# First layer's MLP over both token halves, and the last MLP's first matrix, by seven block products

## The chip, the cores and the metric

One NeuronCore of a Trainium2 chip runs the whole program. The metric is the device time in microseconds (us), here the median of three runs. In the text PE is TensorE (matmuls, weight loads as PEld), DVE is VectorE, ACT is ScalarE, POOL is GpSimd and SP the engine that issues the DMAs.

## The reference

A decoder trunk of two layers over 1024 tokens of width 1024, in float32: an mLSTM layer, then a latent-attention layer, each followed by an MLP of width 4096 with a squared ReLU. Only the MLP and its surroundings are changed:

```python
def sqrelu_mlp(h, w1, w2):
    return jnp.square(jax.nn.relu(h @ w1)) @ w2
...
    for l in range(DEPTH):
        ada = cond @ ada_w[l] + ada_b[l]
        sh1, sc1, g1, sh2, sc2, g2 = jnp.split(ada, 6, axis=-1)
        h = modulate(rmsnorm(x, norm_g[l, 0]), sh1, sc1)
        ...                       # y: the layer's mixer of h (mLSTM or attention)
        x = x + g1[:, None, :] * rmsnorm(y, norm_g[l, 1])
        h = modulate(rmsnorm(x, norm_g[l, 2]), sh2, sc2)
        y = sqrelu_mlp(h, mlp_w1[l], mlp_w2[l])
        x = x + g2[:, None, :] * rmsnorm(y, norm_g[l, 3])
```

## The kernel before, in words

The tokens are worked on in two halves of 512. Activations lie feature-major: a tile holds 128 features on the partitions and 512 tokens along the free dimension. A float32 product is made of three matmuls on parts: each operand is split into a rounded part (hi, type float32r) and the rest (lo), and `mm3` (L230 to L233) issues lo x hi, hi x lo and hi x hi into the same PSUM bank. Weights are loaded by SP into a `raw` buffer of [128, 1024] (four of them), ACT copies the hi part and DVE subtracts for the lo part (`wsplit`, L189 and L190, eight `ws` buffers). Most activations live in 24 `k4` and 8 `hd` buffers of the same size.

`mlp` (from L941) makes one MLP for one half. A hidden column block `f` (32 of 128 columns) takes 8 x 3 matmuls of 512 columns over K = 1024, then ReLU and square on ACT (L957, L958) and a split into hi and lo (`split_mod`, L470 and L471). The second matrix follows behind in groups of G hidden blocks (`up_cols`, or `up_rows`, where the result is wanted with tokens on the partitions), summed into the result in SBUF by DVE (`accumulate`, L198). Steps of both matrices alternate; weights are loaded two steps ahead (AHEAD). A step of 24 matmuls is cut by a "within" in the middle.

The order in time is: mLSTM of both halves; `post`, which adds the residual, takes the norm and leaves the modulated `hf.h2` in parts; then the layer's MLP of half 0, that of half 1 beside the attention of half 0, the last MLP of half 0 beside the attention of half 1, and the last MLP of half 1 alone. `two_streams` weaves them: the mixer yields how many dense steps are to run before it goes on (0.5 is half a step, 12 matmuls; "align" waits for a step of the first matrix), so the yields are the cover behind which a chain of vector work may run. `go` fixes the order of PE's instructions as written; the other engines and the DMA queue are ordered by the scheduler of the framework, by priority (`PRIO` lifts weight loads and evacuations) and by its own estimate of time. Background work (adaLN products `ada_chunk`, rotary tables, latent weights) is stepped from generators: `bgs`, `bg_latent` and `bg_rest`.

Of the kernel before, what the change touches and what calls it, by code (L numbers as in the profile page):

```python
# [9 lines left out]
F32 = mybir.dt.float32  # L10
# [72 lines left out]
def kernel(  # L83
# [145 lines left out]

    def mm3(o, lh, ll, rh, rl, start, stop):  # L230
        nc.tensor.matmul(o, ll, rh, start=start, stop=False)  # L231
        nc.tensor.matmul(o, lh, rl, start=False, stop=False)  # L232
        pe_last[0] = nc.tensor.matmul(o, lh, rh, start=False, stop=stop)  # L233

# [241 lines left out]
    def normed(h, xs_, rstd, A, sh):  # L476

        for k in range(KD):
            with paced():
                nc.vector.scalar_tensor_tensor(  # L480
                    xs_[k], xs_[k], A[:, k : k + 1], rstd, ALU.mult, ALU.mult
                )
                split_mod(h.hi[k], h.lo[k], xs_[k], sh[:, k : k + 1])
            if k % 4 == 3:
                yield 1

# [453 lines left out]

    def mlp(l, hf, y, sizes, rows=False):  # L941


        w1, w2, h = mlp_w1[l], mlp_w2[l], hf.h2
        hids = {}

        def hidden(f):
# [25 lines left out]
        def up_rows(fs, i, last):  # L973
# [40 lines left out]
            def out(ws):  # L1014
                for t in range(t0, t1):
                    if t % 2 == 0:
                        if t > t0:
                            yield "within"
                        b2 = pm()
                    block(b2[:, t % 2], ws, t)  # L1020
# [6 lines left out]
        def up_cols(fs, i, last):  # L1027
# [3 lines left out]
            def out(w):  # L1031
                for m in range(i * n, (i + 1) * n):
                    if m % 2 == 0:
                        if m > i * n:
                            yield "within"
                        b2 = pm()
                    pt = b2[:, m % 2]
                    for q, f in enumerate(fs):
# [6 lines left out]

        up = up_rows if rows else up_cols
        steps, prev, f0 = [], [], 0
        for G in sizes:
# [8 lines left out]
        steps += [up(prev, i, True) for i in range(len(prev))]  # L1057
        ready = []
        for n in range(len(steps) + AHEAD):
            if n < len(steps):  # L1060
                ready.append(steps[n][0]())
            if n >= AHEAD:
                yield from steps[n - AHEAD][1](ready.pop(0))

                yield steps[(n - AHEAD + 1) % len(steps)][1].__name__

# [305 lines left out]
    def prepare_pair(p_, hf):  # L1372
# [61 lines left out]
    def attend(hf, groups, dense, behind=lambda: None):  # L1434
# [46 lines left out]
        us = begin()  # L1481
        yield 1
        while us:
# [4 lines left out]
            for n, work in enumerate(rounds):  # L1488
# [4 lines left out]
                if len(rounds) == 1:  # L1493
                    yield 1
                if n == len(rounds) - 1:
# [6 lines left out]
    def attention_first(hf):  # L1502
# [61 lines left out]
    def x_to_rows(half):  # L1564

        for k in range(KD):
            a, b = tmc(), tmc()
            nc.sync.dma_start(a, xs_blk(k, half))
            yield
            pt = pc()  # L1570
            for t in range(4):
# [178 lines left out]

    def post(hf, y, B, src, A, sh):
        yield from residual(y, hf.i, B, src, (2, 2)[hf.i])
# [3 lines left out]
        rstd = last_of(rs)  # L1756
        yield 0
        hf.h2 = Split()
        yield from normed(hf.h2, y, rstd, A, sh)
# [4 lines left out]
    )  # L1764
    p0 = post(hfs[0], y0, B0, x_ahead(k4v, True), A1, adac(0, SH2))
    so = split_o(hfs[1])
# [81 lines left out]


    p1 = post(hfs[1], y1, B0, x_ahead(hdv, True), A1, adac(0, SH2))  # L1850
    next(p1)
    z0 = FH(claim=True)
    Akv = Aq = B2 = A3 = B3 = None
# [36 lines left out]
    z1 = FH(claim=True)  # L1890
    ya = [None, None]

    def mixer1(hf, z, attention):
# [14 lines left out]
        yield 1  # L1908
        yield from post(hf, y, B2, x_cols, A3, adac(1, SH2))
# [6 lines left out]
    u1 = FH(claim=True)  # L1916

    def all_out():
        yield from x_to_rows(0)
        B3r = along_rows(B3)  # L1920
        yield
        yield from rows_out(hfs[0], u0, B3r)
        yield from x_to_rows(1)
# [39 lines left out]
```

## Time and profile before

| | |
|---|---|
| median of three runs | 2397.75 us (2396.41 to 2398.75) |
| the profiled execution, first to last instruction | 2395.7 us, which is 2.05 us under the median |
| granted TensorE clock, mean | 0.997 |
| DVE busy | 1550.3 us, 65% |
| ACT busy | 1054.9 us, 44% |
| GpSimd busy | 18.3 us, 91 instructions |
| matmuls | 11621 |
| DMA | 374.48 MB, mean 156 GB/s |

No separate time of the profiled execution is given beside its span; what lies around the span is taken as the difference to the median. Busy times of engines overlap each other. The span is cut into 40 slices of some 60 us each; a digit is the busy share in tenths. The busy time of PE counts overlapping matmuls once, so the spacing of matmuls is read from their starts in the timeline.

### The profile page before, as it was taken

How to read it: one execution, taken by the hardware profiler on the slowest of the kernel's cores; microseconds unless marked ns; L12 is line 12 of the kernel's file. 1: busy time of each engine (PE TensorE's matmuls, PEld its weight loads, DVE VectorE, ACT ScalarE, POOL GpSimd, SP SyncE). 2: the span in 40 equal slices, each digit the busy share in tenths (PEclk: the TensorE clock that was granted, in tenths of full speed). 3: DMA queues.
4: the chain of work that ended last, by engine and by line, in shares of the span. 5: the costliest groups of instructions: out<-in, count | busy, mean ns of one | idle time of the engine just before them, and what ended most of it. 6: DMA issues, size and time to landing. Idle time of an engine off the chain costs nothing.

```text
span 2395.7 us, 30518 instructions
## 1 busy us (share of the span) xinstructions
PE 2364.8 (99%) x11621; PEld 1945.5 (81%) x11621; DVE 1550.3 (65%) x2431; ACT 1054.9 (44%) x1712; POOL 18.3 (1%) x91
## 2 busy tenths in 40 slices
PE   7999999999999999999999999999999999999998
PEld 5888888788888887888888877888888888888886
DVE  6667866858656677877764867766566386353345
ACT  4355334655333454444444554344444353443333
POOL 1000000000000000000000000000000000000000
PEclk9999999999999999999999999999999999999999
DMA  8442654544654745545543444864424354354431
GB/s 310 148 143 81 192 178 134 165 132 150 189 171 152 243 138 179 159 160 186 168 137 114 153 162 153 260 240 133 139 97 150 105 167 128 101 189 140 144 99 62
DMA packets 377106, 374.48 MB, mean 156 GB/s; under 512 B 24355, under 2 KB 282464, under 8 KB 376960
## 3 DMA queue, kind: packets, MB, share of 16 engines
q1 hardware_dynamic: 376672, 372.44, 48.9%
q8 instruction: 91, 1.49, 0.3%
q14 instruction: 55, 0.45, 0.1%
q0 software_dynamic: 288, 0.10, 0.0%
HBM read 313.24 MB, written 59.24 MB: 155 GB/s over the span
## 4 chain that ended last, share of the span: by engine, by line
PE 91%; DVE 4%; DMA 3%; ACT 1%; issue 1%; SPq 0%; DVEq 0%; ACTq 0%
PE ps L231 17%; PE ps L232 17%; PE ps L233 17%; PE pm L231 10%; PE pm L232 10%; PE pm L233 10%; PE pc L1445 1%; PE pc L231 1%; PE pc L233 1%; PE pc L232 1%; PE pm L815 1%; PE pm L1331 1%; DMA raw<-in_mlp_w_dram 1%; DVE wl L190 1%; PE pm L1325 1%
## 5 line engine op out<-in xcount | busy, mean ns | idle before, releaser
L190 DVE TENSOR_TENSOR wl<-raw,wh 128x1024 fp32r<-128x1024 f32 (+2 forms) x366 | 438.7, 1202 | 449.5 <-ACT wh L189 442.3
L189 ACT CAST wh<-raw 128x1024 fp32r<-128x1024 f32 (+2 forms) x366 | 376.0, 1032 | 717.0 <-PE ps L231 392.2
L231 PE MATMUL ps<-k,wl 128*128 128x512 f32 x1528 | 611.0, 400 | 2.3 <-ACT k L671 1.4
L233 PE MATMUL ps<-k,wh 128*128 128x512 f32 x1528 | 601.0, 393 | 0.0
L232 PE MATMUL ps<-k,wh 128*128 128x512 f32 x1528 | 600.9, 393 | 0.0
L231 PEld LDWEIGHTS ps<-k,wl 128*128 128x128 f32 x1528 | 287.0, 188 | 69.7 <-issue 2.9
L233 PEld LDWEIGHTS ps<-k,wh 128*128 128x128 f32 x1528 | 287.0, 188 | 67.3 <-issue 0.5
L232 PEld LDWEIGHTS ps<-k,wh 128*128 128x128 f32 x1528 | 287.5, 188 | 63.6 <-issue 1.7
L198 DVE TENSOR_TENSOR k<-k,pm 128x512 f32<-128x512 f32 (+1 forms) x254 | 210.9, 859 | 107.0 <-PE pm L233 106.5
L231 PE MATMUL pm<-hd,wl 128*128 128x512 f32 x512 | 202.0, 394 | 0.4 <-ACT hd L470 0.4
L233 PE MATMUL pm<-hd,wh 128*128 128x512 f32 x512 | 199.8, 391 | 0.0
L232 PE MATMUL pm<-hd,wh 128*128 128x512 f32 x512 | 199.5, 390 | 0.2 <-DVE hd L471 0.2
L231 PE MATMUL pm<-wh,hd 128*128 128x512 f32 x488 | 192.9, 395 | 3.2 <-ACT raw L1337 2.9
L232 PE MATMUL pm<-wl,hd 128*128 128x512 f32 x488 | 191.3, 392 | 0.0
L233 PE MATMUL pm<-wh,hd 128*128 128x512 f32 x488 | 190.3, 390 | 0.0
L360 DVE SCALAR_TENSOR_TENSOR tma<-raw,cond,tma 128x512 f32<-128x512 f32 x168 | 125.6, 747 | 20.6 <-DMA raw<-in_kv_ada_w_dram 14.6
L471 DVE TENSOR_TENSOR hd<-tmp,hd 128x512 fp32r<-128x512 f32 x128 | 88.3, 690 | 56.8 <-ACT hd L470 56.5
L1337 ACT ACTIVATE raw<-pm,sm 128x128 f32<-128x128 f32 (+3 forms) x64 | 47.5, 742 | 151.3 <-DVE sm L1336 122.7
L232 PEld LDWEIGHTS pm<-hd,wh 128*128 128x128 f32 x512 | 96.2, 188 | 21.3 <-DVE hd L471 0.5
L231 PEld LDWEIGHTS pm<-hd,wl 128*128 128x128 f32 x512 | 96.1, 188 | 21.2 <-ACT hd L470 0.8
L233 PEld LDWEIGHTS pm<-hd,wh 128*128 128x128 f32 x512 | 96.1, 188 | 21.1
L231 PEld LDWEIGHTS pm<-wh,hd 128*128 128x128 f32 x488 | 91.6, 188 | 24.9 <-ACT raw L1337 5.5
(347 smaller groups left out, 3414.5 us busy)
## 6 DMA issues: line engine op xcount, KB each, us to landing
raw<-in_mlp_w_dram SPq DMA_DIRECT2D x256, 512.0 KB, 4.1
raw<-in_ada_w_dram SPq DMA_DIRECT2D x80, 512.0 KB, 4.3
raw<-in_a_w_in_dram SPq DMA_DIRECT2D x48, 512.0 KB, 4.1
xs<-k SPq DMA_DIRECT2D x40, 256.0 KB, 4.8
raw<-in_kv_ada_w_dram SPq DMA_DIRECT2D x16, 512.0 KB, 3.8
raw<-in_a_w_out_dram SPq DMA_DIRECT2D x16, 512.0 KB, 4.6
kd<-k SPq DMA_DIRECT2D x32, 256.0 KB, 3.7
vd<-k SPq DMA_DIRECT2D x32, 256.0 KB, 5.0
```

The lines of the kernel that those rows point to most:

```text
L189: nc.scalar.copy(hi[:, :n], r[:, :n])
L190: i = nc.vector.tensor_sub(lo[:, :n], r[:, :n], hi[:, :n].bitcast(F32))
L198: return f(*a, **k)
L231: nc.tensor.matmul(o, ll, rh, start=start, stop=False)
L232: nc.tensor.matmul(o, lh, rl, start=False, stop=False)
L233: pe_last[0] = nc.tensor.matmul(o, lh, rh, start=False, stop=stop)
L360: nc.vector.scalar_tensor_tensor(acc, r[:, kk], cond[:, k : k + 1], acc, ALU.mult, ALU.add)
L471: nc.vector.tensor_sub(lo, u, hi.bitcast(F32))
L815: nc.tensor.matmul(nv[:, r, i], hf.PT[p_][:, r, cs], v[:, 2 * p_ + r], start=g == 0, stop=True,)
L1325: nc.tensor.matmul(o[:, :w], ql, kh, start=True, stop=False)
L1331: nc.tensor.matmul(o[:, :w], qh, kh, start=False, stop=True)
L1337: nc.scalar.activation(pr[:, :n], f, AF.Exp, bias=m, scale=SCALE, accum_out=l)
```

## The change

The product of a 2 x 2 block matrix with another takes eight block products, or seven with sums of blocks before and after. The new `seven` does the latter for a pair of hidden column blocks: the weights' blocks are (two column blocks) x (two halves of K), the tokens' blocks are (two halves of K) x (two sets of tokens). Sums of the weights' blocks are made per pair in `load` by DVE (with `pool`, two of the four by GpSimd), sums of the tokens' blocks once beforehand. Each product is 4 x 3 matmuls; three of the sums afterwards are made by going on accumulating in the same PSUM bank, three by DVE with a copy that ACT kept.

- In layer 0 the two sets of tokens are the two halves (512 columns a matmul). The first ALONE = 6 pairs are still made one half at a time (`up_front`), for half 0 while half 1's `post` runs, for half 1 later, in the stream beside the first attention; the other ten pairs by `seven`, with background steps between the products. `kept0` and `kept1` keep the modulated values whole (`normed_kept`) and make the block sums.
- In the last MLP of half 1 the two sets are its two quarters (256 columns a matmul), all sixteen pairs; `quarters` makes the sums at the end of the attention's `post`.
- The hidden values of these three MLPs go to DRAM (`hidd`), and `mlp(..., stored=True)` then makes the second matrix as a phase of its own with groups of four, fetching and splitting two hidden blocks at a time. The last MLP of half 0 stays as it was.
- The yields of the first attention (`hf.i` = 0) are halved or cut, `bg_rest` runs behind `bg_latent` in the phases of layer 0, and `x_to_rows` of both halves moves into the last MLP's product phase, with its load one block ahead.

The diff, cut to its core:

```diff
+    def split_wide(hi, lo, u):
+        nc.scalar.copy(hi, u)
+        nc.vector.tensor_sub(lo, u, hi.bitcast(F32))
+    def normed_kept(y, rstd, A, sh, parts):
+        for b in range(4):
+            with paced():
+                for k in (2 * b, 2 * b + 1):
+                    nc.vector.scalar_tensor_tensor(
+                        y[k], y[k], A[:, k : k + 1], rstd, ALU.mult, ALU.mult
+                    )
+                    nc.scalar.activation(y[k], y[k], AF.Identity, bias=sh[:, k : k + 1])
+                if parts[b]:
+                    split_wide(*parts[b], y.t[b])
...
+    def up_front(l, hf, pairs):
...
+                s = tmp()
+                with tc.high_priority(PRIO):
+                    nc.scalar.activation(s, pt, AF.Relu)
+                    nc.scalar.activation(s, s, AF.Square)
+                    nc.sync.dma_start(hidd[hf.i, f // 2][:, ts(f % 2, 512)], s)
...
+    def seven(l, pairs, B, out, pool=False):
+        def load(p_):
+            with tc.high_priority(PRIO):
+                r1, r2 = raw(), raw()
+                for r, f in ((r1, 2 * p_), (r2, 2 * p_ + 1)):
+                    nc.sync.dma_start(r.rearrange("p (a b) -> p a b", b=P), wcols(w1, f * P))
+                lo_, hi_ = slice(0, 512), slice(512, 1024)
+                A = wsplit(r1, 1024)
+                t1, t2 = raw(), raw()
+                first = nc.gpsimd if pool else nc.vector
+                first.tensor_add(t2[:, lo_], r2[:, lo_], r2[:, hi_])
+                first.tensor_sub(t1[:, lo_], r1[:, lo_], r2[:, lo_])
+                nc.vector.tensor_sub(t1[:, hi_], t2[:, lo_], r1[:, lo_])
+                nc.vector.tensor_sub(t2[:, hi_], r1[:, hi_], t1[:, hi_])
+                T1 = wsplit(t1, 1024)
+                if pool:
+                    a22, T2 = hd(F32R), (hd(F32R), hd(F32R))
...
+                else:
+                    a22 = sb.tile([P, 1024], F32R, tag="ws", bufs=WS, name=f"wa_{next(uid)}")
+                    T2 = wsplit(t2, 1024)
+                nc.scalar.copy(a22[:, lo_], r2[:, hi_])
+                nc.vector.tensor_sub(a22[:, hi_], r2[:, hi_], a22[:, lo_].bitcast(F32))
...
+        def product(u, i):
+            o = {1: u.b, 6: u.b, 5: u.b, 3: u.b, 2: u.x, 7: u.z, 4: u.z}[i]
+            (wh, wl), (bh, bl) = u.w[i], B[i]
+            for k in range(4):
+                mm3(o, wh[:, k], wl[:, k], bh[k], bl[k], i in (1, 2, 7) and k == 0, k == 3, more=i not in (1, 2, 7))
...
+            for u, i in ((cur, 1), (prev, 5), (cur, 2), (prev, 4), (cur, 6), (prev, 3), (cur, 7)):
+                if u:
+                    product(u, i)
+                    yield "hid"
...
+        def fetch(f):
+            with tc.high_priority(PRIO):
+                r, hi, lo = raw(), k4v(F32R), k4v(F32R)
+                nc.sync.dma_start(r, hidd[hf.i, f // 2])
+                split_wide(hi, lo, r.rearrange("p (a b) -> p a b", b=512))
...
-        yield 1
+        yield (0.5, 1)[hf.i]                      # prepare_pair; the same twice in attend
...
-            yield 2
+            yield 1
...
-                hf, groups, cycle((1,)),
+                hf, groups, cycle((0.5,)),        # attention_first
...
-    f0 = mlp(0, hfs[0], z0, [4] * 8)
-    for n in range(20):
-        if next(f0) != "within":
+    for v in up_front(0, hfs[0], range(ALONE)):
+        if v != "within":
+            next(p1, None)
             next(p1, None)
     drain(p1)
-    two_streams(f0, behind(bg_latent(), 4))
+    bgl = chain(bg_latent(), bg_rest())
+    z0 = FH()
+    f2 = mlp(0, hfs[0], z0, [], stored=True)
+    f0, n = seven(0, range(ALONE, NF // 2), blocks, both_halves), 0
+    while go(f0) is not end:
...
+        next(bgl, None)
+        if n == 7 * (NF // 2 - ALONE) - 5:
+            next(f2)
...
+    two_streams(with_b12(f2), behind(bgl, 1))
...
-    two_streams(mlp(0, hfs[1], z1, [2] * 14 + [4]), mixer1(hfs[0], z0, attention_first), bg_rest())
+    two_streams(
+        chain(
+            up_front(0, hfs[1], range(ALONE)),
+            (v for v in mlp(0, hfs[1], z1, [], stored=True) if v != "primed"),
+        ),
+        mixer1(hfs[0], z0, attention_first), bgl,
+    )
...
-    dense = mlp(1, hfs[1], u1, [4] * 8, True)
+    dense, n = seven(1, range(NF // 2), blocks1, one_half(hfs[1]), True), 0
+    while go(dense) is not end:
+        n += 1
+        if n % 3 == 0 and v != "rows":
+            v = next(fill)
+    u1 = FH()
+    dense = mlp(1, hfs[1], u1, [], True, True)
```

More of the change, by code (lines that the diff above doesn't have):

```diff
@@ L228, with mm3 @@
     pe_last = [None]
[L230 to L233, printed above, removed]
+    def mm3(o, lh, ll, rh, rl, start, stop, more=False):
+        m = dict(skip_group_check=True) if more else {}
+        nc.tensor.matmul(o, ll, rh, start=start, stop=False, **m)
+        nc.tensor.matmul(o, lh, rl, start=False, stop=False, **m)
+        pe_last[0] = nc.tensor.matmul(o, lh, rh, start=False, stop=stop, **m)
     nc.scalar.preload_act_table_set("natural_log_exp_and_others")
@@ L939, with ahead_of @@
     AHEAD = 2
-    def mlp(l, hf, y, sizes, rows=False):
+    hidd = scratch([2, NF // 2, P, 2 * H], "hidd")
+    def ahead_of(steps, primed=False):
+        ready = []
+        for n in range(len(steps) + AHEAD):
+            if primed and n == AHEAD:
+                yield "primed"
+            if n < len(steps):
+                ready.append(steps[n][0]())
+            if n >= AHEAD:
+                yield from steps[n - AHEAD][1](ready.pop(0))
+                yield steps[(n - AHEAD + 1) % len(steps)][1].__name__
@@ L1046, in mlp, with both @@
         up = up_rows if rows else up_cols
+        if stored:
+            fetch(0)
+            fetch(2)
+            steps = []
+            for g in range(NF // 4):
+                for i in range(4):
+                    load, run = up(list(range(4 * g, 4 * g + 4)), i, g == NF // 4 - 1)
+                    def both(load=load, f=4 * g + 2 * i):
+                        w = load()
+                        if i >= 2 and f < NF:
+                            fetch(f)
+                        return w
+                    steps.append((both, run))
+            n = 0
+            for v in ahead_of(steps, True):
+                if v == "primed":
+                    yield v
+                    continue
+                n += v != "within"
+                yield v if v == "within" else "hid"
+            return
         steps, prev, f0 = [], [], 0
@@ L1057, in mlp @@
         steps += [up(prev, i, True) for i in range(len(prev))]
[L1058 to L1065, printed above, removed]
+        yield from ahead_of(steps)
     rope_d = scratch([2, P, S], "rope_d")
@@ L1481, in attend @@
         us = begin()
-        yield 1
+        yield (0.5, 1)[hf.i]
         while us:
@@ L1757, in post @@
         yield 0
+        if kept:
+            yield from kept(y, rstd)
+            return
         hf.h2 = Split()
```

207 lines of the change are left out of this document (194 added, 13 removed).

## The prediction, made before the run

> **What bounds the kernel now.** I read the page from its engines, over the forty slices, to the chain that ended last; then the groups of instructions with their shapes kept apart, then windows and the timeline where the change lands.
>
> ```profile
> PE 2364.8 (99%) x11621; PEld 1945.5 (81%) x11621; DVE 1550.3 (65%) x2431; ACT 1054.9 (44%) x1712; POOL 18.3 (1%) x91
> ...
> PE   7999999999999999999999999999999999999998
> ...
> PEclk9999999999999999999999999999999999999999
> ...
> PE 91%; DVE 4%; DMA 3%; ACT 1%; issue 1%; SPq 0%; DVEq 0%; ACTq 0%
> PE ps L231 17%; PE ps L232 17%; PE ps L233 17%; PE pm L231 10%; PE pm L232 10%; PE pm L233 10%; PE pc L1445 1%; PE pc L231 1%; PE pc L233 1%; PE pc L232 1%; PE pm L815 1%; PE pm L1331 1%; DMA raw<-in_mlp_w_dram 1%; DVE wl L190 1%; PE pm L1325 1%
> ```
>
> TensorE is busy 99% of the span at full granted clock, is 91% of the chain, and some 81% of the chain are the three matmul lines of mm3. So the time is a count of matmuls times their spacing, and a change pays by what it takes out of that count, less what it lets TensorE wait. The busy column can't give the spacing, since neighbours overlap; the timeline does, by starts.
>
> ```profile
> 317.16 0.28 PE L231 MATMUL ps<-wh,k 128*128 128x256 f32 x1
> ...
> 321.75 0.28 PE L231 MATMUL ps<-wh,k 128*128 128x256 f32 x1
> ...
> 1110.71 0.39 PE L231 MATMUL ps<-k,wl 128*128 128x512 f32 x1
> ...
> 1116.27 0.39 PE L231 MATMUL pm<-hd,wl 128*128 128x512 f32 x1
> ```
>
> From the third row to the fourth 24 matmuls of 512 columns start, 5.56 us, so 0.2317 us each. From the first to the second 39 matmuls of 256 columns start, 4.59 us, so 0.1177 us each, each with a weight load of its own: half as wide costs 51%.
>
> **The change: matmuls.** Layer 0's first matrix takes 2 x 768 matmuls of 512. After: six pairs of columns per half in the old way (2 x 288), ten pairs over both halves in seven products of 12 instead of eight (10 x 84 = 840); 1416 in all, 120 fewer, 120 x 0.2317 = 27.8 us. The last MLP's first matrix, 768 of 512 = 177.9 us, becomes 16 x 84 = 1344 of 256, x 0.1177 = 158.2 us: 19.7 us. Second matrices keep their 768 a piece. Together 47.5 us of TensorE's time. What follows is what the vector side charges for it.
>
> ```profile
> L190 DVE TENSOR_TENSOR wl<-raw,wh 128x1024 fp32r<-128x1024 f32 x350 | 426.6, 1222 | 444.5 <-ACT wh L189 440.1 <-PE ps L233 2.9 <-DMA lw<-wl 0.9
> L360 DVE SCALAR_TENSOR_TENSOR tma<-raw,cond,tma 128x512 f32<-128x512 f32 x168 | 125.6, 747 | 20.6 <-DMA raw<-in_kv_ada_w_dram 14.6 <-DMA raw<-in_ada_w_dram 4.3
> L198 DVE TENSOR_TENSOR k<-k,pm 128x512 f32<-128x512 f32 x170 | 108.9, 682 | 54.2 <-PE pm L233 53.7
> L471 DVE TENSOR_TENSOR hd<-tmp,hd 128x512 fp32r<-128x512 f32 x128 | 88.3, 690 | 56.8 <-ACT hd L470 56.5
> L457 DVE TENSOR_TENSOR tmc<-tmc,tmc 128x512 f32<-128x512 f32 x90 | 62.0, 689 | 7.1 <-ACT tmc L453 5.3
> L358 DVE TENSOR_SCALAR tma<-raw,cond 128x512 f32<-128x512 f32 x24 | 11.5, 478 | 3.8 <-DMA raw<-in_kv_ada_w_dram 3.6 <-DMA raw<-in_ada_w_dram 0.3
> L661 DVE COPY k<-ps 128x256 f32<-128x256 f32 x16 | 6.7, 420 | 5.1 <-PE ps L233 5.1
> L1339 DVE TENSOR_SCALAR raw<-raw,sm 128x1024 f32<-128x1024 f32 x8 | 6.0, 754 | 0.6
> ...
> L189 ACT CAST wh<-raw 128x1024 fp32r<-128x1024 f32 x350 | 365.3, 1048 | 708.4 <-PE ps L231 391.8 <-DMA raw<-in_mlp_w_dram 101.4 <-PE pm L231 80.4
> ...
> L612 POOL MEMSET raw<- 128x1024 f32 x2 | 1.9, 954 | 146.9 <-DVE wl L190 146.9
> ...
> raw<-in_mlp_w_dram SPq DMA_DIRECT2D x256, 512.0 KB, 4.1
> ```
>
> **Layer 0's ten pairs.** VectorE per pair: three weight splits (3 x 1.22), four block sums (4 x 0.69), the seventh block's rest (0.69), three adds out of PSUM (3 x 0.68), two ReLUs (0.75 + 0.48): 10.4 us. Seven steps of the background come beside it; a chunk of the adaLN product has seven steps and 0.48 + 7 x 0.75 = 5.7 us. So 16.1 us against 84 x 0.2317 = 19.5 us of TensorE, 83%.
>
> ```profile
> 495.00:566.00 71.00, 71.00 (x307) 57.25 (x306) 53.61 (x77) 42.20 (x61) 0.55 (x4) 1.00 0.44 139
> 960.00:1200.00 240.00, 239.21 (x1239) 200.03 (x1238) 185.83 (x325) 101.19 (x188) 2.87 (x14) 1.00 0.54 170
> 1560.00:1860.00 300.00, 295.69 (x1626) 250.82 (x1625) 186.40 (x304) 128.54 (x217) 3.60 (x20) 1.00 0.46 153
> 1920.00:1980.00 60.00, 60.00 (x263) 48.64 (x262) 55.90 (x81) 33.12 (x49) 0.20 (x2) 1.00 0.49 159
> ```
>
> (The columns are the window, its length, then busy time and count of PE, PEld, DVE, ACT and POOL, the clock, the DMA share, GB/s.) The last window had VectorE at 93% with TensorE never idle, so 83% is covered; I charge 2 us, between 0 and one 1.2 us instruction in the way in each of ten pairs.
>
> **Getting there.** The block sums of the tokens must be ready before the third product. The first column of the old first matrix starts at 492.38 in the trace and half 1's last square is added by 495.05:
>
> ```profile
> 492.38 0.39 PE L231 MATMUL ps<-k,wl 128*128 128x512 f32 x1
> ...
> 494.36 0.69 DVE L457 TENSOR_TENSOR tmc<-tmc,tmc 128x512 f32<-128x512 f32 x1
> ...
> 1124.94 0.36 PE L1331 MATMUL pm<-k,k 128*128 128x256 f32 x1
> ...
> 1128.92 0.35 DVE L1339 TENSOR_SCALAR raw<-raw,sm 128x256 f32<-128x256 f32 x1
> ...
> 1130.70 1.04 PE L1445 MATMUL pc<-ident,raw 128*128 128x128 f32 x8
> ```
>
> From there VectorE has two reciprocal roots (8 x 0.69), the residual (8 x 0.75 + 8 x 0.69), seven sums of squares (4.8), the norm (8 x 0.75) and eighteen wide operations of sums and splits (18 x 1.22): some 50 us; ten weight splits, 12 us; the first pair's weights, 3 x 1.22 + 5 x 0.69 = 7 us. That is 69 us, to 564. TensorE has twelve columns (12 x 5.56) and two products (5.6), to 565. It just fits if VectorE never idles; in the old chain's window, 495 to 566, it idled 17.4 of 71 us. So 0 to 16 us of waiting, and I take 6: the pacing of one step per column made part of the old idling, and the steps now come two per column.
>
> **Attention of half 0.** Its dense cover falls from 1536 matmuls to 1056, and most yields of the pairs are halved, so 12 matmuls (2.78 us) stand where 24 stood. In the first round of a pair the last score starts at 1124.94, the last scaling ends at 1129.27, and TensorE comes to the transposes at 1130.70; with 2.78 us less it comes at 1127.92 and waits 1.35 us. The second attention (1560 to 1860), which has half steps already, idles 4.3 of 300 us against 0.8 of 240 in the first. Four pairs with one such wait: 5.4 us, with three waits each 16 us, with VectorE relieved of G=2's extra adds perhaps none. I take 6. Its dense work also ends nearly with the mixer, so the norm ahead of the last layer's MLP loses cover: 2 us, at most one step's 5.6.
>
> **The last MLP's sixteen pairs.** Here a pair has only 84 x 0.1177 = 9.9 us. VectorE: three splits 3.67, two sums 1.38, the seventh block 0.69, three adds of 256 (3 x 0.42), one ReLU 0.75: 7.75 us, 78%. GpSimd has two sums of 512, an operation that the trace lacks; its write of 1024 took 0.95 us, so not under 0.48 us each, and I put the upper end at twice VectorE's 0.69. If they run beside VectorE nothing is lost; one after the other it is 8.7 to 10.5 us per pair, up to 0.6 over. I take 6 us for the stage, half of that and a little for the short slack of a product (1.4 us) against a 1.05 us ScalarE copy in the way.
>
> **Hidden by cover.** The hidden values' way through DRAM: 60 stores and 48 loads, about 50 MB on top of 374, and 20 weight loads fewer; the mean of 156 GB/s rises to about 175. A store lands tens of us before its load. The 48 wide splits after the load (59 us of VectorE) replace 96 splits of 0.69 at L471 (66 us).
>
> The sum: span 2395.7 - 47.5 + 2 + 6 + 6 + 2 + 6 = 2370.2; the span shown lies 2.05 under the median, so 2372 us.
>
> **Rivals.** (1) All new waits are hidden, as nearly all were before: 2397.75 - 47.5 = 2350 us. For it: the slices of nines. Against: the 1.35 us worked out above.
>
> (2) VectorE and GpSimd exclude each other in the last MLP. By rows: a two-input operation of VectorE stands still while GpSimd's runs and the other way round, so a pair costs 10.5 us and, with each delay passed on to the weight splits, up to 1.5 us over TensorE's 9.9: 24 us in place of 6, so 2390 us. Nothing in this trace shows it, as GpSimd here only writes. The Trainium skill, page "SBUF — State Buffer", section "Who interferes with whom", states just this: a VectorE instruction with two SBUF inputs and a GpSimd instruction that reads SBUF hold a shared port in turn, each for its whole length. No run here has tested it.
>
> (3) Slower: the weights of the last MLP's pairs become a chain. A pair needs all four raw buffers: two landings (4.1 us), GpSimd's two sums (1 to 2.8), two sums (1.4), then copy (1.05) and three splits in turn (1.22, 1.22, 0.69): 10.7 to 12.5 us from issue to the release of the second buffer. If the next pair's loads wait for that release, sixteen pairs at 12.5 cost 42 us over TensorE's 9.9, in place of 6: 2408 us. It decides from 12 us per pair on. Against: the first buffer is free after the sums, so two pairs can overlap.
>
> (4) A 256-column matmul is bound by its weights.
>
> ```profile
> L231 PEld LDWEIGHTS ps<-k,wl 128*128 128x128 f32 x1528 | 287.0, 188 | 69.7 <-issue 2.9
> ```
>
> At 0.188 us a load, 1344 would take 253 us and the kernel 2465. The 39 matmuls at 0.1177 speak plainly against it.
>
> **How the numbers follow.** Forecast 50%, its own range 2358 to 2385; (1) 20%; (2) 15%; (3) 13%; (4) 2%. The range 2345 to 2402 leaves out (4), most of (3)'s upper half, and what lies 5 us and more under (1), the vector work saved being no more than that in the places where TensorE waits. A measurement here tells 0.2%, 4.8 us, from no change: faster 0.83 (forecast, (1) and nearly all of (2)), same 0.05 (the edges of (2) and (3)), slower 0.12.
>
> **What would show it.** Matmul count down to some 12,080 (120 fewer of 512, 768 of 512 gone, 1344 of 256 new). The spacing of the new 256s at 0.118. Between two pairs of the last MLP 9.9 to 10.5 us; 12 or more speaks for (3), a VectorE two-input operation of 512 longer than 0.69 there for (2). An idle of TensorE ended by VectorE once at some 565 us, and of about 1.3 us ahead of L1445's successors in each pair of the first attention. I am wrong if the idle time of TensorE grows by over 47 us, or the 256s space out.

## The result, and the profile after

The changed kernel takes 2524.68 us (median of four runs, 2523.22 to 2532.22) against 2397.40 for the kernel before on the same chip: ratio 1.0531, 95% interval 1.0513 to 1.0548. It is 127 us slower where 25 us faster were forecast. The profiled execution took 2524.39 us, its span 2522.5. Here is its page: busy time by engine, the forty slices, the DMA total, the chain that ended last, and the costliest groups.

```profile
PE 2367.9 (94%) x12077; PEld 1961.3 (78%) x12077; DVE 1746.8 (69%) x2643; ACT 1129.4 (45%) x1770; POOL 64.5 (3%) x111
...
PE   8999999998996998798999989999999999898998
...
PEclk9999999999998999799999989999999999999999
...
DMA packets 386524, 441.71 MB, mean 175 GB/s; under 512 B 26595, under 2 KB 278560, under 8 KB 386368
...
PE 69%; DMA 13%; DVE 11%; ACT 3%; issue 3%; POOL 0%; SPq 0%; DVEq 0%; ACTq 0%; POOLq 0%
...
L490 DVE TENSOR_TENSOR k<-raw,k 128x1024 fp32r<-128x1024 f32 x98 | 119.6, 1224 | 95.7 <-ACT k L489 94.3
...
L489 ACT CAST k<-raw 128x1024 fp32r<-128x1024 f32 x98 | 102.5, 1050 | 143.6 <-DMA raw<-hidd 139.4
...
raw<-hidd SPq DMA_DIRECT2D x96, 512.0 KB, 4.4
```

Of the matmuls all came as forecast: 12077. (By the code four of the seven products, not three as the section on the change says, go on accumulating in a bank that another has begun.) The new ones of 256 columns have the spacing of the old: in the timeline twenty of them start from the first to the second row here, 2.35 us, 0.1175 each.

```profile
2199.80 0.28 PE L232 MATMUL ps<-k,wl 128*128 128x256 f32 x1
...
2202.15 0.28 PE L234 MATMUL ps<-k,hd 128*128 128x256 f32 x1
```

So the 47.5 us of matmul time are saved, and TensorE loses some 175 us more than before. Of these 124 are idle time (the span less PE's busy time: 30.9 us before, 154.6 after), where the prediction called itself wrong from 47 on. The rest lies within what the page counts as busy, in part as matmuls at a lower clock (last section). PE fell from 91% of the chain to 69%, and DMA and DVE stand there with 13% and 11%. The last row of the first fence is the one to remember: 96 loads of hidden values, where the prediction counted 48.

To place the loss, the timeline has a mark in each stage: the two matmuls with a tile of ones that sum the squares of a residual stream (L461 before, L462 after). The three marks below end the first layer's MLP of half 0, the first attention with the MLP of half 1, and the second attention. Before:

```profile
866.70 1.02 PE L461 MATMUL pc<-tmc,ones 128*128 128x512 f32 x2
...
1411.38 1.02 PE L461 MATMUL pc<-tmc,ones 128*128 128x512 f32 x2
...
1958.52 1.02 PE L461 MATMUL pc<-tmc,ones 128*128 128x512 f32 x2
```

After:

```profile
1048.59 1.02 PE L462 MATMUL pc<-tmc,ones 128*128 128x512 f32 x2
...
1520.20 1.02 PE L462 MATMUL pc<-tmc,ones 128*128 128x512 f32 x2
...
2067.13 1.02 PE L462 MATMUL pc<-tmc,ones 128*128 128x512 f32 x2
```

By the count of matmuls the first stage has 360 more of 512 (+83.4 us), the second 480 fewer (-111.2), the tail 19.7 us less. Loss is what lies over that:

| stage | before | by count | after | loss | forecast loss |
|---|---|---|---|---|---|
| to the first mark | 866.7 | 950.1 | 1048.6 | 98.5 | 8 |
| first attention | 544.7 | 433.5 | 471.6 | 38.1 | 8 |
| second attention | 547.1 | 547.1 | 546.9 | 0 | 0 |
| last MLP of half 1, to the end | 437.2 | 417.5 | 455.4 | 37.9 | 6 |

What TensorE waited for stands in the view of waits with TensorE's rows alone (columns: waiting matmul, releaser, us in total, times, longest). First the first stage, from 530 to 1048 us, a window in which TensorE is busy for 446.8 of 518 us (in the kernel before, for all of it):

```profile
PE pc L341 <- DVE tma L361: 22.0, 3, 8.4
PE pm L232 <- ACT k L202: 9.7, 1, 9.7
PE ps L232 <- DVE wl L190: 7.5, 3, 4.4
PE ps L233 <- DVE hd L490: 6.3, 1, 6.3
...
PE pc L1386 <- DVE tma L1378: 5.5, 1, 5.5
```

Then the first attention's, from 1049 to 1520:

```profile
PE pm L232 <- ACT k L489: 9.4, 2, 5.4
PE pm L232 <- ACT raw L1569: 8.4, 8, 1.3
PE pm L233 <- DVE k L490: 5.1, 2, 4.0
```

And the tail, from 2067 on:

```profile
PE pm L232 <- DVE hd L1042: 15.2, 12, 2.6
```

L341 and L1386 are transposes of background work (an adaLN vector, a bias of the latent weights): they stand in TensorE's queue, and no matmul ran past them, until VectorE had finished the sum that they transpose. L489 and L490 split a fetched pair of hidden values; L202 empties a PSUM tile, on ScalarE, which ahead of it had stood 7.2 us for a block of the background's weights (L1381) and then, at L489, 4.8 us for a fetch. L1042 is an addition of the last MLP's products.

### The profile page after: what moved, and what is told of

The parts are those of the page before. It is cut to its first block, busy times and chain, and to the rows that moved or that the text cites. A ratio compares the mean times of both kernels' runs of the same rounds, so it can differ in the third digit from the quotient of the medians.

```text
span 2522.5 us, 32315 instructions
## 1 busy us (share of the span) xinstructions
PE 2367.9 (94%) x12077; PEld 1961.3 (78%) x12077; DVE 1746.8 (69%) x2643; ACT 1129.4 (45%) x1770; POOL 64.5 (3%) x111
## 4 chain that ended last, share of the span: by engine, by line
PE 69%; DMA 13%; DVE 11%; ACT 3%; issue 3%; POOL 0%; SPq 0%; DVEq 0%; ACTq 0%; POOLq 0%
PE ps L232 12%; PE ps L233 12%; PE ps L234 12%; PE pm L232 8%; PE pm L233 8%; PE pm L234 7%; DMA raw<-in_mlp_w_dram 5%; DMA raw<-hidd 4%; DVE wl L190 2%; DVE k L490 1%; DVE tma L361 1%; PE pc L1677 1%; ACT wh L189 1%; DMA raw<-in_ada_w_dram 1%; PE pc L233 1%
## 5 line engine op out<-in xcount | busy, mean ns | idle before, releaser
L232 PE MATMUL ps<-k,wl 128*128 128x512 f32 (+1 forms) x1200 | 470.6, 392 | 19.0 <-DVE wl L190 10.1
L234 PE MATMUL ps<-k,wh 128*128 128x512 f32 (+1 forms) x1200 | 461.4, 384 | 0.0
L233 PE MATMUL ps<-k,wh 128*128 128x512 f32 (+1 forms) x1180 | 454.0, 385 | 0.0
L232 PE MATMUL pm<-k,wl 128*128 128x512 f32 (+1 forms) x764 | 298.2, 390 | 63.5 <-DVE hd L1042 15.2
L233 PE MATMUL pm<-k,wh 128*128 128x512 f32 (+1 forms) x764 | 292.6, 383 | 6.0 <-DVE k L490 6.0
L234 PE MATMUL pm<-k,wh 128*128 128x512 f32 (+1 forms) x764 | 291.3, 381 | 0.0
L234 PEld LDWEIGHTS ps<-k,wh 128*128 128x128 f32 x1200 | 228.8, 191 | 47.6 <-issue 0.5
L233 PEld LDWEIGHTS ps<-k,wh 128*128 128x128 f32 x1180 | 225.2, 191 | 44.6 <-issue 2.4
L232 PEld LDWEIGHTS pm<-k,wl 128*128 128x128 f32 x764 | 147.4, 193 | 101.9 <-DVE hd L1042 18.5
L490 DVE TENSOR_TENSOR k<-raw,k 128x1024 fp32r<-128x1024 f32 x98 | 119.6, 1224 | 95.7 <-ACT k L489 94.3
L233 PEld LDWEIGHTS pm<-k,wh 128*128 128x128 f32 x764 | 147.4, 193 | 36.9 <-DVE k L490 7.7
L234 PEld LDWEIGHTS pm<-k,wh 128*128 128x128 f32 x764 | 147.5, 193 | 28.1
L489 ACT CAST k<-raw 128x1024 fp32r<-128x1024 f32 x98 | 102.5, 1050 | 143.6 <-DMA raw<-hidd 139.4
L361 DVE SCALAR_TENSOR_TENSOR tma<-raw,cond,tma 128x512 f32<-128x512 f32 x168 | 125.8, 749 | 24.7 <-DMA raw<-in_ada_w_dram 12.7
L232 PE MATMUL pm<-wh,hd 128*128 128x512 f32 x256 | 101.9, 398 | 4.7 <-ACT raw L1569 2.6
L1569 ACT ACTIVATE raw<-pm,sm 128x128 f32<-128x128 f32 (+3 forms) x64 | 47.4, 741 | 130.2 <-DVE sm L1568 127.9
L234 PE MATMUL pm<-wh,hd 128*128 128x512 f32 x256 | 100.0, 391 | 0.0
```

Of the source, the lines that this page charges most:

```text
L232: nc.tensor.matmul(o, ll, rh, start=start, stop=False, **m)
L233: nc.tensor.matmul(o, lh, rl, start=False, stop=False, **m)
L361: nc.vector.scalar_tensor_tensor(acc, r[:, kk], cond[:, k : k + 1], acc, ALU.mult, ALU.add)
L489: nc.scalar.copy(hi, u)
L490: nc.vector.tensor_sub(lo, u, hi.bitcast(F32))
L1569: nc.scalar.activation(pr[:, :n], f, AF.Exp, bias=m, scale=SCALE, accum_out=l)
```

## Experiments: which part, which stage

**One part at a time.** In e1 the last MLP is as in the kernel before, in e2 the first layer.

```diff
 e1: -    dense, n = seven(1, range(NF // 2), blocks1, one_half(hfs[1]), True), 0
     +    dense = mlp(1, hfs[1], u1, [4] * 8, True)
 e2: -    f0, n = seven(0, range(ALONE, NF // 2), blocks, both_halves), 0
     +    f0 = mlp(0, hfs[0], z0, [4] * 8)
```

> Only layer 0's part of the change; the last MLP, the loading of its rows and its tail are as before. Between the same landmarks in the two traces the last MLP's part cost 18 us (437.2 to 455.4) and all before it 109 us. If the two parts act each for itself, this runs at 2524.7 - 18 = 2506 us. Rival: the loss is of something that both share (the buffers in DRAM, the order of the queue), and with one part gone the other loses much less: under 2480 us.

> Only the last MLP's part of the change on the kernel before. If the parts are independent: 2397.4 + 18 = 2415 us, with about 12.1 us between two pairs of column blocks in the product phase, as in the changed kernel, where 84 matmuls need 9.9. Rival: the product phase is slowed by what layer 0's part leaves behind; then about 2380 us.

Measured: e1 2506.32 us, ratio 1.0445 (1.0403 to 1.0487), 105.6 us over before; e2 2419.84, 1.0085 (1.0062 to 1.0108), 19.1 over. Their sum, 124.7, is the 127.3 of the whole within the runs' scatter: the parts do not act on each other, and each is a loss.

**Uncovered background.** After half 0's second matrix three adaLN chunks ran with nothing beside them; in the window from 1003 to 1030 us TensorE was busy for 3.73 of 27 us; the second row is the change from the products to the second matrix (columns: window, length, busy time and count of PE, PEld, DVE, ACT, POOL, clock, DMA share, GB/s).

```profile
1003.00:1030.00 27.00, 3.73 (x13) 2.58 (x14) 20.09 (x34) 2.09 (x2) 0.00 (x0) 0.51 0.76 234
780.00:840.00 60.00, 37.27 (x137) 27.98 (x136) 42.94 (x61) 26.96 (x28) 0.00 (x0) 0.77 0.88 298
```

```diff
 e3: -    two_streams(with_b12(f2), behind(bgl, 1))
     +    two_streams(with_b12(f2), behind(bgl, 2))
 e8: -    bgl = chain(bg_latent(), bg_rest())
     +    bgl = bg_latent()
     -        mixer1(hfs[0], z0, attention_first), bgl,
     +        mixer1(hfs[0], z0, attention_first), bg_rest(),
```

> The changed kernel, with two background steps instead of one for each dense step beside half 0's second matrix. Theory: three adaLN chunks were left over when the dense work ended there and ran alone, 7.9 us each with TensorE idle (1003 to 1030 us): that goes, 25 to 30 us, so about 2497 us. Rival: raw buffers and VectorE are the limit in that stage anyway and denser background only moves the idling forward: within 8 us of 2525, or slower.

> The whole change (2524.7 us), with the adaLN vectors' background work beside the first attention again, as in the kernel before, instead of behind the latent weights in the first layer's MLP. Theory: the three chunks that ran alone after half 0's second matrix, about 25 us of TensorE waiting, go, as they did with two background steps at a time (2501 us): 2497 to 2502 us. Rival: the first attention pays for them in its own waits, since its PSUM tiles and SP's queue are now busy with the second matrix of half 1 too: 2515 us or more.

Measured: e3 2501.25 us (ratio 1.0424, 1.038 to 1.0467), 23 us better, a little under the 25 to 30 expected. e8 2512.64 (1.0467, 1.0443 to 1.0491), between theory and rival: its first mark comes at 1002.0 us, 46.6 earlier, but the first attention's stage takes 506.3 us instead of 471.6, so 34.7 are paid back there. Moving the background pays only where there is cover for it.

## Experiments: the last MLP

**The shared port.** In this stage VectorE's first sum took 2.6 times as long as the next, which has the same shape and operands, while GpSimd's second sum ran (the view of single lines, here L1010 to L1013 between 2154 and 2335 us; columns: count, shortest/median/longest ns).

```profile
L1011 POOL TENSOR_TENSOR raw<-raw,raw x13: 1274/1622/1749, 2156.0 to 2303.8; 128x512 f32<-128x512 f32 x13
...
L1012 DVE TENSOR_TENSOR raw<-raw,raw x13: 1746/1778/1791, 2156.4 to 2304.3; 128x512 f32<-128x512 f32 x13
...
L1013 DVE TENSOR_TENSOR raw<-raw,raw x13: 691/692/695, 2158.2 to 2306.1; 128x512 f32<-128x512 f32 x13
```

That is the rule of the Trainium skill that rival 2 rests on (page "SBUF — State Buffer", section "Who interferes with whom"); the trace agrees, 1.78 us against 0.69. Whether it bounds the stage, e4 asks, with all sums on VectorE.

```diff
-                first = nc.gpsimd if pool else nc.vector
+                first = nc.vector
```

> The changed kernel, with all four sums of the last MLP's weights on VectorE, none on GpSimd. Theory (a chain of loads through four raw buffers, 12.1 us a pair): GpSimd's two sums of 1.3 to 1.8 us and VectorE's third sum, held up to 1.78 us by the second, become three of 0.69: the chain is 2.7 us shorter, about 9.4 us, and TensorE bounds again near 10 to 10.5: 16 x 1.6 to 2 = 25 to 32 us less, about 2496 us. Rival (VectorE's own work is the bound): it grows from 7.75 to 9.1 us a pair, and the stage gains under 8 us or loses.

Measured: 2528.13 us, ratio 1.0536 (1.0499 to 1.0572), no gain, though L1012 now took 0.684 us in all 13. The contention is real, but this run does not price it: with GpSimd's two sums taken over, VectorE's work per pair stays nearly the same, 9.0 us by its rows against 9.3. What it speaks against is the theory that the loads' chain goes through GpSimd.

**Tiles.** The pool `hd` has eight tiles, and a pair takes four (output, a22, both parts of T2). In e2's waits VectorE's L1018, the low part of T2, waits for a product of the pair before to give up its `hd` slot, and the addition L1042 stands behind it in VectorE's queue. e5 takes the output from `k4`; e6 takes three `raw` tiles per pair instead of four, by writing T2's sums over r2 once a22 has been split; e7 does both. All three stand on e2.

```diff
 e5: -            o, s = Half(), hdv()
     +            o, s = Half(), k4v()
 e6: -                t1, t2 = raw(), raw()
     +                t1 = raw()
     ...
     +                nc.scalar.copy(a22[:, lo_], r2[:, hi_])
     +                first.tensor_add(r2[:, lo_], r2[:, lo_], r2[:, hi_])
     +                nc.vector.tensor_sub(a22[:, hi_], r2[:, hi_], a22[:, lo_].bitcast(F32))
```

> Only the last MLP's part of the change (2419.8 us), and in it the tile for a pair's four output blocks is taken from the pool k4 instead of hd, so that hd serves three tiles per pair instead of four. Theory A (buffers of hd: the low part of T2 waits for a product of the previous pair to free its slot, c00's addition queues behind it on VectorE, and TensorE waits for that addition, 27 us summed in the last MLP's rows): most of these waits go, 2397 to 2405 us. Theory B (the three-deep chain of the raw tiles behind the weight loads) and theory C (the order of the work on VectorE itself): 2414 us or more.

> Only the last MLP's part of the change (2419.8 us), and in it a pair takes three raw tiles instead of four: the sums of the block T2 are written over r2, after the block a22 has been split. Theory B (a load can be issued only when the previous pair's sums and splits have released a raw tile; SP's queue waited 24.8 us for it in 13 pairs): 2400 to 2406 us. Theory A: within 6 us of 2419.8.

> Only the last MLP's part of the change, with both edits: the output tile from k4 and three raw tiles per pair. If A and B each hold a share of the 22 us by which this part is slower than the kernel before: 2385 to 2398 us, so no slower than before. If only one of them is the cause, the time of that one alone (2397 to 2406 us). If the order on VectorE is the cause (theory C): 2412 us or more.

Measured: e5 2406.05 us (ratio 1.0029, 1.0017 to 1.0042), 14 better than e2; e6 2421.84 (1.0094, 1.0074 to 1.0113), nothing; e7 2387.59, ratio 0.9951 (0.9931 to 0.997), 32 better than e2 and 12 better than the kernel before (2399.37 there). The tile of `hd` holds 14 us by itself; e6's edit holds nothing by itself, and 18 once that tile is mended. Waits between 2045 and 2205 us, first of e2, TensorE's longest and VectorE's for the slot:

```profile
PE pm L232 <- DVE hd L1042: 14.6, 12, 3.4
DVE hd L1018 <- PE pm L234: 10.6, 11, 2.5
```

Then of e5, where the wait for L1042 is gone and another took its place: ScalarE waits in its queue for the last sum of T2 (L1013), and the copy L1048, which TensorE needs, stands behind.

```profile
ACT hd L1017 <- DVE raw L1013: 54.4, 13, 5.6
...
PE pm L232 <- ACT tmc L1048: 10.4, 10, 2.5
```

And e7, where the longest of TensorE's that is left is one wait, and VectorE's sum L1018 now waits for GpSimd's:

```profile
DVE raw L1018 <- POOL raw L1016: 28.0, 12, 3.6
...
PE ps L232 <- DVE k L1052: 1.5, 1, 1.5
```

The stores of the pairs (sixteen; the row gives the first and last start) show the period: e6 (2238.0 - 2050.8) / 15 = 12.5 us, e5 11.3, after 12.1, e7 10.5, close to 84 x 0.1177 (9.9) and four transposes of x_to_rows.

```profile
L1086 SPq DMA_DIRECT2D hidd<-k x16: 319/379/572, 2045.1 to 2203.2; - x16
```

e6's edit changes more than the number of raw tiles: the order on ScalarE and VectorE too, and with it the contention ends. The sum that took 1.78 us in e2 (L1012) waits for GpSimd in e6 and e7 (L1018 there) and then takes 0.69. The runs do not part these three. So the price of the contention stays open; they show only that its end brings nothing while the wait for `hd` is there (e4, e6).

## Experiments: the first layer

**Together.** e9 has e7's two edits in the whole change, and e3's.

> The whole change with the three edits that gained so far: the last MLP's output tile from k4 and three raw tiles per pair (32 us in the last MLP's part alone), and two background steps per dense step beside half 0's second matrix (23 us). If the parts are independent: 2524.7 - 32 - 23 = 2469 to 2473 us. If the last MLP's edits act on the first layer's ten pairs too (three raw tiles there as well): down to 2455 us.

Measured: 2464.14 us, ratio 1.0265 (1.0243 to 1.0287), 5 us under the range for independent parts and above the 2455 for parts that act on one another. The marks show both: the tail is 28.6 us shorter than in the kernel after (426.8 against 455.4), and the first stage ends at 1015.7, 12.9 us ahead of e3, which has the two steps as well, so the three raw tiles act on the first layer's pairs too. Three guesses followed on what holds the rest, all on e9.

```diff
 e10: +        if n < 7 * (NF // 2 - ALONE) - 12:
              next(bgl, None)
      -        if n == 7 * (NF // 2 - ALONE) - 5:
      +        if n == 7 * (NF // 2 - ALONE) - 12:
      ...
      -    two_streams(with_b12(f2), behind(bgl, 2))
      +    two_streams(with_b12(f2), behind(bgl, 3))
 e11: -                    nc.scalar.activation(u.to.c[0][1], u.b, AF.Relu)
      +                    nc.vector.tensor_scalar(u.to.c[0][1], u.b, 0.0, None, ALU.max)
 e12: e10 and e11, and
      +            if n == 4 * ALONE - 4:
      +                next(g)         # g: the second matrix of half 1, at its first fetches
```

> As the run before, and in the first layer's block products the background (latent weights) takes no step in the last two rounds of seven products, the first fetches of the second matrix's values are issued there instead, and the background then takes three steps per dense step. Theory: TensorE's 27 us of waits between 785 and 830 us come from the latent weights' raw tiles and SP's queue standing before the second matrix's first loads and fetches: 15 to 25 us less than the run before. Rival: the waits only move into the stretch where three steps now crowd beside the second matrix: within 6 us of the run before.

> As the first run of this call, and the ReLU that empties a pair's last PSUM block runs on VectorE instead of ScalarE, in both places of the block products. Theory: next pair's first product waits for this ReLU, which stands behind weight copies in ScalarE's queue (about 10 us in the ten pairs of the first layer): 6 to 10 us less than the first run. Rival: VectorE's queue is as late: within 4 us, or slower in the last MLP, where VectorE has the most work.

> The two edits of the two runs before together, and the fetches of the second matrix of half 1 issued four loads before its first product (they cost 4 to 6 us of waiting at the start of the first attention's stage). If each acts alone: the sum of their gains on the first run of this call less another 4 to 6 us, 2430 to 2445 us; if the waits only change places: 2455 to 2470 us. In neither case faster than the kernel before.

Measured: e10 2476.61 us (ratio 1.0318, 1.0298 to 1.0338), e11 2470.82 (1.0301, 1.0272 to 1.033), e12 2482.66 (1.0357, 1.0329 to 1.0386): all slower than e9. e11 loses its 7 us in the last MLP, as its rival had it (that stage takes 435.5 us against e9's 426.8). e10 and e12 are slower even than their rivals said (within 6 us of e9, and 2455 to 2470): the waits did not only change places, they grew. In e10 the same waits came back later, with the three steps:

```profile
PE pm L232 <- ACT k L489: 11.7, 5, 4.6
PE pc L1388 <- DVE tma L1380: 9.3, 4, 4.7
PE pm L233 <- DVE k L490: 8.1, 8, 2.5
PE pc L341 <- DVE tma L361: 7.4, 2, 6.0
```

**The background itself, and the raw tiles.** All on e9.

```diff
 e13:      bgl = chain(bg_latent(), bg_rest())
      +    drain(bgl)
 e14: RAW 4 -> 5, TMP 3 -> 2, TMC 6 -> 5
 e15: TMP 3 -> 2, TMC 6 -> 5
 e16: -        next(bgl, None)
      +        if n < 7 * (NF // 2 - ALONE) - 12:
      +            some(bgl, 1 + n % 2)
```

> As e9 (2464 us), with all of the background work (latent weights, adaLN vectors) done by itself before the first layer's seven products, and none beside them or beside half 0's second matrix. Theory (background): TensorE's waits from there to the end of half 0's second matrix fall from some 50 us in e9 to under 20, the rest being the block sums at the start (6) and the fetches; the time as a whole is that of e9 less these 30 us plus what the background takes alone, which no run has shown. Rival (the products' own weights and buffers): 35 us or more of waits stay.

> As e9, with five raw tiles in the pool instead of four; for the room TMP goes from 3 to 2 and TMC from 6 to 5. Theory (raw tiles): 10 to 25 us less than the control e15, at the change to the second matrix and at the starts of the fetches above all. Rival: within 5 us of the control.

> The control: as e9, with TMP 2 and TMC 5 and four raw tiles. 0 to 15 us more than e9's 2464, for the attention stages use these tiles.

> As e9, with one or two background steps in turn beside each of the first 57 of the 70 products, none beside the last 13, and the first fetches issued at the beginning of those. Theory (the background at the change to the second matrix costs 20 to 30 us there): 10 to 20 us less than e9. Rival (the waits go along with the steps): within 5 us of e9 or slower, with the waits now beside the products, before 750 us.

Measured: e13 2560.20 us (ratio 1.0677, 1.0656 to 1.0698), e14 2460.95 (1.0265, 1.0245 to 1.0286), e15 2467.14 (1.028, 1.0256 to 1.0304), e16 2500.78 (1.0429, 1.0404 to 1.0453). A fifth raw tile is 6 us better than its control, which is within the control's own scatter (2460.27 to 2467.84), and not the 10 to 25 of the theory. e16 is 37 us slower than e9: TensorE is idle for 28.7 us from 563 to 750 instead of 11.6, the waits having gone along with the steps, and from 750 to 850 for 35.6 instead of 23.0. The answer is in e13's windows, the first with the background alone (and, at its end, the last block sums and the first pair's weights, for which TensorE waits 9.1 us), the second with the ten pairs and the whole second matrix of half 0:

```profile
563.00:720.00 157.00, 17.26 (x57) 10.83 (x58) 135.54 (x235) 20.08 (x22) 0.00 (x0) 0.51 0.73 237
720.00:1112.00 392.00, 389.76 (x1679) 316.28 (x1678) 219.77 (x237) 160.68 (x185) 0.00 (x0) 0.99 0.50 162
```

Without background beside it TensorE is busy for 389.76 of 392 us: the seven products, their sums, the change to the second matrix and the fetches cost nothing by themselves. The background alone is some 148 of the 157 us, mostly VectorE's work. The kernel has to lay it beside 392 us of matmuls in which VectorE already has 220. e9 does it in 452 us, at a price of some 60, of which 10 are the background's own transposes on TensorE:

```profile
563.00:1015.00 452.00, 408.16 (x1729) 324.33 (x1728) 344.93 (x474) 175.24 (x200) 0.00 (x0) 0.95 0.69 228
```

**Fetched twice.** The 96 loads led back to the code. The loading function of a step is made in a loop and called when the loop is over:

```python
            for g in range(NF // 4):
                for i in range(4):
                    ...
                    def both(load=load, f=4 * g + 2 * i):
                        w = load()
                        if i >= 2 and f < NF:
                            fetch(f)
```

`f` is bound when the function is made, `i` is looked up when it is called, and is then 3 for all. So every step fetches, each pair of values comes twice, and the second copy, the one used, is asked for only one or two steps ahead of its product; as the condition places it, it would be three or four. e17 binds `i` on the kernel after, e18 on e9.

```diff
-                    def both(load=load, f=4 * g + 2 * i):
+                    def both(load=load, f=4 * g + 2 * i, i=i):
```

> The whole change, with each pair of hidden values fetched from DRAM and split once instead of twice (48 fetches instead of 96), and at the step where the code's condition places it. Theory: 48 loads of 512 KB, 48 copies of 1.05 us on ScalarE and 48 splits of 1.22 us on VectorE (50 and 59 us) go, and with them the waits for a fetch (L489 and L490, some 45 us in the kernel after) and part of the contention of the background for raw tiles: 2475 to 2495 us instead of 2524.7. Rival: the double fetch is hidden, as TensorE's waits come from the background and the products alone: 2515 us or more.

> e9 (2464 us: output tile in k4, three raw tiles, two background steps at a time) with each pair fetched once. Theory: a gain of 25 to 40 us, 2424 to 2439 us; it still isn't faster than the kernel before, since the background beside the first layer's products stays. Rival as for the run before: within 8 us of 2464.

Measured: e17 2487.87 us, ratio 1.037 (1.0353 to 1.0387), 37 us better than the kernel after; e18 2429.55, ratio 1.0129 (1.0114 to 1.0144), 35 better than e9. As the theory had it. The edit halves the fetches and gives each a longer lead; the runs do not part the two. The page of e17, its rows for the split and the loads:

```profile
L490 DVE TENSOR_TENSOR k<-raw,k 128x1024 fp32r<-128x1024 f32 x50 | 60.9, 1224 | 42.6 <-ACT k L489 41.7
...
raw<-hidd SPq DMA_DIRECT2D x48, 512.0 KB, 3.7
```

e18's marks, for the stages of the table above:

```profile
1003.18 1.02 PE L462 MATMUL pc<-tmc,ones 128*128 128x512 f32 x2
...
1451.69 1.02 PE L462 MATMUL pc<-tmc,ones 128*128 128x512 f32 x2
...
1998.96 1.02 PE L462 MATMUL pc<-tmc,ones 128*128 128x512 f32 x2
```

Its losses are 53.1 us in the first stage (1003.2 - 950.1), 15.0 in the first attention's (448.5 - 433.5) and 10.7 in the tail (428.2 - 417.5; span 2427.2): 78.8 in place of 174.5. TensorE's longest wait left in the first stage, from 530 to 1003 us:

```profile
PE pm L232 <- ACT k L202: 11.2, 1, 11.2
```

So this wait isn't one for a second copy: ScalarE's copy L202 there stands behind the copy of a weight that had waited 5.97 us for its load. The block sums' wait (5.0 us) and smaller ones are beside it. That they come of the background follows from e13, where, with none beside the matmuls, one wait of 2.2 us is left; no run shows it on e18 itself. Taking the background out of the products altogether (e13) costs more.

## Why the prediction was wrong

- **The matmul term held.** 120 of 512 fewer, 768 of 512 replaced by 1344 of 256, spacing 0.1175: 47.5 us. Rival 4 is out (its 2465 should be 2467 by its own terms).
- **"Hidden by cover" failed, in its count.** "60 stores and 48 loads", "48 wide splits": there are 96 loads and 96 wide splits; the count was taken from what the code says and not from what it issues. That is 59 us of VectorE and 50 of ScalarE more, and 37 us of the time (e17, with the longer lead). e13 kept the 96 and lost nothing in half 0's second matrix, so the double fetch costs where it meets the background and the attention.
- **"Layer 0's ten pairs", 2 us, failed in what it covered.** Per pair the vector work did fit, as e13 shows. What I left out is how many background steps remain when the pairs are through, that they stand beside the second matrix alone, and that their transposes hold TensorE's queue. The adaLN steps had stood beside the first attention, with 480 more matmuls there; put back beside what is left, they cost 34.7 us (e8). Of the 98.5 us in that stage, two steps at a time gave back 20 (e3's mark at 1028.6), fetching once 14 (e17's at 1034.7) and three raw tiles 13 (e9 against e3).
- **"Getting there", 6 us, was right**: one wait of 6.3 us ended by VectorE, at 573 us (L490 in the waits).
- **"Attention of half 0", 6 + 2 us, became 38.** The waits of 1.3 us came, two per pair and 8.4 us in all, but of a dense matmul for the PSUM tile that the exponential (L1569) still read, not of the transposes. Most of the rest were the fetches: 9.4 + 5.1 us of waits, and 22 us of the stage went with them in e17 (449.2 us). With one fetch per pair 15 are left.
- **"The last MLP's sixteen pairs", 6 us, became 38.** VectorE's work per pair was 9.3 us by its rows instead of 7.75 (L1012 1.78 for 0.69, L1023 0.97 for 0.69, L1082 1.00 for 0.75), still under TensorE's 9.9. The price of rival 3 was right (12 us per pair; 12.1 measured), but not its mechanism: freeing a raw tile earlier alone gave nothing (e6). It was slots of `hd` and what e6's edit changes, one wait behind the other (e5, e7). With both mended the tail is 428.2 us in e7 (span 2385.0 less its mark at 1956.8), 11 over the count where 6 were foretold, and VectorE's work there is 7.7 us per pair.
- **Rival 2's contention** exists; whether it has a share in the last MLP's loss stays open, since e4 gave its work to VectorE and e6's edit ended it along with two other things. **Rival 1** needed all waits hidden; it came closest in e7, whose part alone saved 12 of its 19.7 us.

The range's upper end took in one mechanism of a loss at a time. Four came together, in different stages, and they added.

## What to carry to other kernels

When a change takes matmuls out, list the work that was hidden behind them and find its new cover first, its transposes in TensorE's queue included; the background alone, drained in one run, tells most of its bill. Count DMAs and splits in the trace of the first run against the count that the code intends: 96 for 48 stood in one row of the page. When one mended wait brings nothing, look for the wait that stands behind it, and mend both before dropping either.

## What the runs showed of the hardware

Waits cost more than their length. In the timeline of the kernel after, TensorE waits 4.00 us for a fetch, one matmul later 1.15 us more, and then works at little over half speed: from 1155.14 to 1159.83 eleven matmuls of 512 start, 0.426 us each instead of 0.2317. The granted clock is 0.52 from 1154 to 1161.

```profile
1148.52 0.40 PE L234 MATMUL ps<-k,wh 128*128 128x512 f32 x1
1152.91 0.49 PE L232 MATMUL pm<-k,wl 128*128 128x512 f32 x1 [4.00 <-ACT k L489]
...
1155.14 0.63 PE L234 MATMUL pm<-k,wh 128*128 128x512 f32 x1
...
1159.83 0.63 PE L233 MATMUL pm<-k,wh 128*128 128x512 f32 x1
```

Counted over all starts of 256 and 512 columns, 261 matmuls of the kernel after have between 1.55 and 2.1 times the usual spacing, and 104 of the kernel before; beyond the usual spacing these take 36.7 and 12.7 us. So some 24 of the 175 us may be put down to this slow restart. The Trainium skill, page "TensorE: Matmul & The Clock Gate", Part 1, gives 426.7 ns for 512 columns at the halved clock, and the trace agrees with 0.426. The page has the clock fall after at least one idle window of about 3.4 us. In the last MLP it also came behind a wait of 1.83 us; the wait before that one, of 1.28 us, ended twelve us earlier. There the trace differs from the page, for no idle time of 3.4 us stands ahead:

```profile
2204.26 0.63 PE L1810 MATMUL pc<-ident,tmc 128*128 128x128 f32 x4 [1.83 <-DMA tmc<-xs]
...
2205.34 0.41 PE L232 MATMUL pm<-k,wl 128*128 128x256 f32 x1
...
2208.32 0.40 PE L234 MATMUL ps<-k,wh 128*128 128x256 f32 x1
```

From the second row to the third fourteen matmuls of 256 start, 2.98 us, 0.213 each instead of 0.1175: at least 1.3 us on top of the wait. The granted clock is 0.55 from 2204.8 to 2208.5, after 1.00 from 2196 to 2202.
